# Masking inside the running sum, and VectorE turning the last sixteen keys of each query tile

## The chip, the cores and the metric

The kernel runs on one core of a Trainium2 chip. The metric is the device time of one execution in microseconds. The core's engines have queues of their own: TensorE (PE in the profile; its weight loads are PEld), VectorE (DVE), ScalarE (ACT), GpSimd (POOL) and SyncE (SP, which issues transfers). A profile is one execution recorded instruction by instruction.

## The reference

One layer of a streaming encoder on 512 positions with 16 learned tokens in front (528 keys), width 1024, all in float32. A normalised input is projected to two attention branches of eight heads each; both are merged by gates, projected, added, and followed by a gated feed-forward layer and a last norm. The stick-breaking branch is

```
z = einsum('bhqd,bhkd->bhqk', q, k) * 128 ** -0.5
causal = kpos < qpos
u = where(causal, log_sigmoid(-z), 0)
rest = cumsum(u, axis=3, reverse=True) - u
a = where(causal, exp(log_sigmoid(z) + rest), 0)
o = a @ v
```

So each weight depends on the sum over all later keys that are still before the query, and keys at or behind the query have weight zero. The second branch (differential attention) takes two softmax maps with a bias by distance, subtracts them and weights v in the same way.

## The kernel before

The queries are the 512 real positions, in four tiles of 128; tile t sees the keys 0 to 144 + 128 t. Float32 products are made of three products of split operands (`mm3`, lines 287 to 292: high by high, high by low, low by high).

**The loop over heads.** First eight stick-breaking heads (`sb_head`), then eight differential ones (`df_head`). A head is a generator: it makes its scores, its weights, turns them, and multiplies by v. Each `yield n` lets n units of other work go in between: the projections of the next head's q, k and v, output projections of earlier heads, gates. `weights` prepares the split of projection weights some units ahead (L78 on ScalarE, L79 on VectorE). A planner then fixes each engine's queue: it goes through simulated time and gives a free engine the ready instruction that stands first in the program; instructions inside `tc.high_priority` (evacuations of units) count as 150 places earlier. Only the beginning, up to `order.close()`, is in the order written. On the chip each engine works through its queue in order and waits by semaphores.

**Scores (lines 616 to 626).** Each tile's scores for stick-breaking go to two PSUM tiles of two banks: zA holds tiles 0, 1 (bank 0, columns 0 to 416) and 2 (bank 1), zB tile 3. Each of the four diagonal blocks gets one more product, L620: a bf16 identity times `mask_b`, a constant of 0 and -1e30, which is added to the scores.

**Weights (lines 627 to 641).** s = softplus(z) by three ScalarE activations (L632 to L634) and L635 on VectorE; L639 sums s backwards in place by four scans a head (144, 272, 416 and 528 columns) that add and start from 0; L640 and L641 give exp(z - sum).

**Turning (`attn_out`, lines 545 to 575).** To multiply by v, weights have to lie with keys on the partitions. `turn(j, pt)` transposes key block j of all query tiles that see it on TensorE into one PSUM bank (L556) and splits it into `a_h` (L558, ScalarE) and `a_l` (L559, VectorE). `turn_first` does blocks 0 and 1. One unit later `turn_rest` does block 2 in a third bank, and in a fourth bank `pt` the diagonal block of tile 3 (L568) and the sixteen keys behind each query tile: four small transposes (L571) that place tile t's keys at partitions 32 t. L572 copies the diagonal block to `a_f`; L575 copies the sixteen rows of each tile to `a_s`, two on ScalarE and two on VectorE. Only the last queries of a tile see these keys: 32 in stick-breaking (`lo_rows` 96), 64 in differential heads. `a_s` is zero elsewhere. `weighted` multiplies a_h and a_l with the split v, then a_f (L583) and a_s (L584) with v in plain float32; the matching rows of v come from `v_s` (L537). In a stick-breaking head the four banks are the two halves of two z tiles (from a pool of two), so blocks 0 and 2 share one tile; in a differential head they are four tiles of a pool of four.

**Other parts that matter here.** `bias` (L700, GpSimd) holds a differential head's distance term in the buffer of tag `bias`; L711 on VectorE adds it to the scores. GpSimd's queue also starts many transfers (L145, L690, L801, L803).

Of the kernel before, what the change touches and what calls it, by code (L numbers as in the profile page):

```python
# [9 lines left out]
F32 = mybir.dt.float32  # L10
# [31 lines left out]
def block_kernel(ctx: ExitStack, tc: tile.TileContext, x, meta, norm_mix_g, w_in, w_gate, b_gate,  # L42
# [316 lines left out]
    ident = const.tile([P, P], F32, name="ident")  # L359
    make_identity(nc, ident)  # L360

    mask_b = const.tile([P, 144], BF16, name="mask_b")

    dist = const.tile([P, L], F32, name="dist")
    ident_b = const.tile([P, P], BF16, name="ident_b")
    ones_r = const.tile([P, P], F32R, name="ones_r")
    eps_t = const.tile([P, 1], F32, name="eps_t")
    pcol = const.tile([P, 33], F32, name="pcol")
# [34 lines left out]

    a_s = ap_.tile([P, 256], F32, name="a_s")
    nc.gpsimd.memset(a_s, 0.0)

    def kv_units(key, evac):
        def unit(hf):
# [113 lines left out]
    def v_units(key, d):  # L522
        vT = d["vT"] = ap_.tile([P, L], F32, tag="vT", bufs=1, name="vT")

        def turn():

            vf = ap_.tile([P, 2, P], F32, tag="vf", bufs=2, name="vf")
            vh = ap_.tile([P, 3, P], F32R, tag="vh", bufs=2, name="vh")
            vl = ap_.tile([P, 3, P], F32R, tag="vl", bufs=2, name="vl")
            pt, p5 = tr_tile(), tr_tile()  # L530
            for j in range(4):
                nc.tensor.transpose(pt[:, j * P:(j + 1) * P], vT[:, j * P:(j + 1) * P], ident)  # L532
            pv = pt.rearrange("p (j c) -> p j c", c=P)
            nc.scalar.copy(vh, pv[:, 0:3])
            nc.vector.tensor_tensor(vl, pv[:, 0:3], vh.bitcast(F32), op=ALU.subtract)
            nc.scalar.copy(vf[:, 0], pt[:, 3 * P:4 * P])
            nc.scalar.copy(v_s.rearrange("p (t q) -> p t q", q=32)[:, :, 0:NM],  # L537
                           vT[:, NM:L].rearrange("p (t q) -> p t q", q=P)[:, :, P - NM:P])
            nc.tensor.transpose(p5[:, 0:P], v_s, ident)
            nc.scalar.copy(vf[:, 1], p5[:, 0:P])  # L540
            d["v"] = (vf, vh, vl)

        return kv_units(key, lambda ps, s: nc.scalar.copy(vT[:, s], ps)), turn

    def attn_out(blocks, d, lo_rows, banks):
# [7 lines left out]
        def turn(j, pt):  # L553
            n = 512 - j * P
            for t in range(j, NQ):
                nc.tensor.transpose(pt[:, (t - j) * P:(t - j + 1) * P], blocks(t, j * P, (j + 1) * P), ident)  # L556
            c = slice(off[j], off[j] + n)
            nc.scalar.copy(a_h[:, c], pt[:, 0:n])  # L558
            nc.vector.tensor_tensor(a_l[:, c], pt[:, 0:n], a_h[:, c].bitcast(F32), op=ALU.subtract)  # L559

        def turn_first():
            for j, pt in enumerate(banks()):
                turn(j, pt)

        def turn_rest():
            p2, pt = banks()
            turn(2, p2)
            nc.tensor.transpose(pt[:, 384:512], blocks(3, 3 * P, 4 * P), ident)  # L568
            for t in range(NQ):
                b = blocks(t, (t + 1) * P - 32 * t, (t + 1) * P + NM)  # L570
                nc.tensor.transpose(pt[0:32 * t + NM, t * qn:(t + 1) * qn], b[lo_rows:P], ident[lo_rows:P, lo_rows:P])  # L571
            nc.scalar.copy(a_f, pt[:, 384:512])  # L572
            for t in range(NQ):
                r, c = slice(32 * t, 32 * t + NM), slice(t * qn, (t + 1) * qn)
                (nc.scalar.copy if t < 2 else nc.vector.tensor_copy)(a_s[r, c], pt[r, c])  # L575

        def weighted():
            vf, vh, vl = d["v"]
# [32 lines left out]
    def sb_head(h, d, o_h, o_l):  # L611
# [1 line left out]
        kh, kl = d["k"]  # L613
        zA, zB = z_tile(), z_tile()

        def score(o, t, k0, k1, mo, mn):
            q = slice(t * P, (t + 1) * P)
            mm3(o, [(qh[:, q], ql[:, q], kh[:, k0:k1], kl[:, k0:k1])], stop=(mn == 0))
            if mn:
                nc.tensor.matmul(o[:, mo:mo + mn], lhsT=ident_b, rhs=mask_b[:, 0:mn], start=False, stop=True)  # L620

        score(zA[:, 0, 0:256], 0, 0, 256, NM, P)
        score(zA[:, 0, 144:416], 1, 0, 272, NM + P, P)
        score(zA[:, 1, 0:416], 2, 0, 416, NM + 2 * P, 144)
        score(zB[:, 0, 0:HL], 3, 0, HL, 0, 0)
        score(zB[:, 1, 0:HL], 3, HL, L, 400 - HL, P)
        res = []
        for z, n in ((zA, 416), (zB, HL)):
            zz = z[:, :, 0:n]
# [4 lines left out]
            nc.scalar.activation(e, e, AF.Ln, bias=1.0)  # L634
            nc.vector.scalar_tensor_tensor(s, zz, 0.0, e, op0=ALU.max, op1=ALU.add)  # L635
            sf = s.rearrange("p a b -> p (a b)")
            for a, b in (((0, 144), (144, 416), (416, 832)) if n == 416 else ((0, L),)):
                f = sf[:, a:b][:, ::-1]
                nc.vector.tensor_tensor_scan(f, f, f, 0.0, op0=ALU.add, op1=ALU.bypass)  # L639
            nc.vector.tensor_tensor(s, zz, s, op=ALU.subtract)  # L640
            nc.scalar.activation(s, s, AF.Exp)  # L641
            res.append(sf)
        base = ((0, 0), (0, 144), (0, 416), (1, 0))
        zs = []

        def banks():
            if zs:
                return [z[:, 1] for z in zs]
            zs.extend((z_tile(), z_tile()))
            return [z[:, 0] for z in zs]  # L650

# [45 lines left out]
    def df_head(h, d, o_h, o_l):  # L697
# [53 lines left out]
        yield 1  # L751
        scores3(1)
        maps(3)
        t1, t2, av = attn_out(lambda t, k0, k1: prs[t][:, 0, k0:k1], d, 64, lambda: (tr_tile(), tr_tile()))
        yield 3 if h < NH - 1 else 2
        t1()
        yield 1
# [228 lines left out]
    for k in range(KT):  # L986
# [10 lines left out]
    pm = mm_tile()  # L997
    nc.tensor.transpose(pm[:, 0:33], prow, ident[0:33, 0:33])
    nc.vector.tensor_copy(pcol[:, 8:33], pm[:, 8:33])
    nc.gpsimd.memset(mask_b, 0.0)  # L1000
    nc.gpsimd.affine_select(out=mask_b, in_=mask_b, pattern=[[-1, 144]], compare_op=ALU.is_gt,
                            fill=-BIG, base=0, channel_multiplier=1)
    nc.vector.tensor_copy(ones_r, onesf)
    nc.vector.tensor_copy(ident_b, ident)
    order.close()
    units[5]()
    turn()
# [527 lines left out]
```

## Time and profile before

| | |
|---|---|
| median of 3 runs | 954.66 us (953.51 to 954.71) |
| the profiled execution | 955.27 us |
| its span in the trace | 953.5 us |
| TensorE busy | 940.6 us (99%), granted clock 0.998 |
| VectorE busy | 720.8 us (76%) |
| ScalarE busy | 592.8 us (62%) |
| GpSimd busy | 190.5 us (20%) |
| stick-breaking heads' scans (L639) | from 41.3 us on |
| differential heads, first bias read (L711) | 262.9 us |

A row of a group or of the timeline names the line, the engine, the operation, the tile written and the tiles read, and the shape. Times of products overlap, because they are pipelined; the distance between two starts tells what a product costs when the queue is full. In brackets stands the idle time of the engine ahead of an instruction, and what ended it.

### The profile page before, as it was taken

What the parts mean: (1) busy time and instruction counts of PE and PEld (TensorE: products, weight loads), DVE (VectorE), ACT (ScalarE), POOL (GpSimd) and SP (SyncE); (2) the same over time, 40 slices, a digit from 0 to 9 for tenths busy, and PEclk for the clock granted to TensorE, in tenths of its full rate; (3) what the DMA queues carried; (4) which work ended last, traced back from release to release, by engine and by line L of the source; (5) the groups of instructions that cost most, each with busy time, mean ns of one, the idle gap of its engine ahead of it and who ended that gap; (6) DMA issues with size and microseconds to landing.
All of it is one profiled execution on the core that took longest, in us unless ns stands there. A gap on an engine that the chain in (4) does not pass through costs nothing.

```text
span 953.5 us, 16249 instructions
## 1 busy us (share of the span) xinstructions
PE 940.6 (99%) x6105; PEld 851.1 (89%) x6106; DVE 720.8 (76%) x1336; ACT 592.8 (62%) x1137; POOL 190.5 (20%) x212
## 2 busy tenths in 40 slices
PE   8999999999999999999999999999999999999996
PEld 5988989898999899998987888899999999988886
DVE  7978777765677666876662578899888888989875
ACT  7765676666566666666676356765555555666654
POOL 3200121222133343344513530001000000000013
PEclk9999999999999999999999999999999999999999
DMA  8525678778777879799987865527743343276642
GB/s 246 154 63 149 164 176 204 159 166 228 198 178 174 213 170 185 181 204 180 199 198 168 260 197 170 150 78 171 155 123 111 90 120 103 67 255 203 198 151 89
DMA packets 155824, 158.42 MB, mean 166 GB/s; under 512 B 6465, under 2 KB 117218, under 8 KB 155746
## 3 DMA queue, kind: packets, MB, share of 16 engines
q1 hardware_dynamic: 132690, 101.61, 35.5%
q0 software_dynamic: 22896, 55.72, 28.6%
q8 instruction: 48, 0.79, 0.3%
q14 instruction: 30, 0.25, 0.1%
q10 hardware_dynamic: 160, 0.07, 0.0%
HBM read 133.64 MB, written 50.86 MB: 193 GB/s over the span
## 4 chain that ended last, share of the span: by engine, by line
PE 90%; DVE 6%; ACT 2%; issue 1%; DMA 1%; ACTq 0%; DVEq 0%
PE mm L290 21%; PE mm L291 21%; PE mm L292 21%; PE z L290 6%; PE z L291 6%; PE z L292 6%; PE z L708 1%; PE z L707 1%; DVE wl L79 1%; PE tr L556 1%; PE tr L532 1%; PE z L556 1%; DMA slots<-in_w_ffn_down_dram 1%; PE z L584 1%; DVE hres L1212 1%
## 5 line engine op out<-in xcount | busy, mean ns | idle before, releaser
L290 PE MATMUL mm<-xT_h,wh 128*128 128x264 f32 (+2 forms) x656 | 214.5, 327 | 0.5 <-ACT xT_h L912 0.5
L291 PE MATMUL mm<-xT_l,wh 128*128 128x264 f32 (+2 forms) x656 | 213.4, 325 | 0.5
L292 PE MATMUL mm<-xT_h,wl 128*128 128x264 f32 (+2 forms) x656 | 212.5, 324 | 0.0
L79 DVE TENSOR_TENSOR wl<-wst,wh 128x1024 fp32r<-128x1024 f32 (+1 forms) x147 | 164.2, 1120 | 44.9 <-ACT wh L78 44.7
L78 ACT CAST wh<-wst 128x1024 fp32r<-128x1024 f32 (+1 forms) x147 | 141.6, 965 | 84.7 <-PE mm L291 62.5
L291 PEld LDWEIGHTS mm<-xT_l,wh 128*128 128x128 f32 x656 | 123.5, 188 | 10.1 <-DVE xT_l L913 1.3
L290 PEld LDWEIGHTS mm<-xT_h,wh 128*128 128x128 f32 x656 | 123.5, 188 | 10.0 <-ACT xT_h L912 0.9
L292 PEld LDWEIGHTS mm<-xT_h,wl 128*128 128x128 f32 x656 | 123.4, 188 | 10.0
L290 PE MATMUL mm<-hT_h,wh 128*128 128x256 f32 x304 | 85.7, 284 | 0.4 <-ACT hT_h L1169 0.4
L292 PE MATMUL mm<-hT_h,wl 128*128 128x256 f32 x304 | 86.0, 284 | 0.0
L291 PE MATMUL mm<-hT_l,wh 128*128 128x256 f32 x304 | 86.0, 283 | 0.0
L290 PEld LDWEIGHTS mm<-hT_h,wh 128*128 128x128 f32 x304 | 57.3, 189 | 0.6 <-ACT hT_h L1169 0.6
L291 PEld LDWEIGHTS mm<-hT_l,wh 128*128 128x128 f32 x304 | 57.6, 190 | 0.0
L292 PEld LDWEIGHTS mm<-hT_h,wl 128*128 128x128 f32 x304 | 57.4, 189 | 0.0
L711 DVE CUSTOM_DVE_ANT_0 pr<-z,bias 128x144 f32<-128x144 f32 (+3 forms) x64 | 30.9, 501 | 35.0 <-PE z L708 34.9
L290 PE MATMUL mm<-o_h,wh 128*128 128x512 f32 x128 | 53.2, 416 | 0.0
L1437 POOL TENSOR_TENSOR outs<-hres,gF 128x512 f32<-128x512 f32 x4 | 6.2, 1554 | 226.0 <-DVE hres L1423 217.8
L291 PE MATMUL z<-wl,da 128*128 128x512 f32 (+1 forms) x132 | 50.4, 381 | 0.3 <-DVE wl L79 0.3
L145 POOL DMA_DIRECT2D ds<-in_w_ffn_down_dram x36 | 30.1, 840 | 102.3 <-ACT wh L78 68.6
L291 PE MATMUL mm<-o_l,wh 128*128 128x512 f32 x128 | 50.1, 392 | 0.3 <-DVE o_l L779 0.3
L290 PE MATMUL z<-wh,da 128*128 128x512 f32 (+1 forms) x132 | 50.2, 381 | 0.0
L292 PE MATMUL z<-wh,da 128*128 128x512 f32 (+1 forms) x132 | 50.2, 380 | 0.0
(375 smaller groups left out, 2554.4 us busy)
## 6 DMA issues: line engine op xcount, KB each, us to landing
wst<-in_w_in_dram SPq DMA_DIRECT2D x40, 512.0 KB, 5.7
ds<-in_w_ffn_down_dram POOLq DMA_DIRECT2D x30, 512.0 KB, 6.2
wst<-in_w_ffn_gate_dram SPq DMA_DIRECT2D x22, 512.0 KB, 4.0
wsu<-in_w_ffn_up_dram SPq DMA_DIRECT2D x20, 512.0 KB, 3.8
wst<-in_w_gate_dram SPq DMA_DIRECT2D x16, 512.0 KB, 6.8
y_df<-y_out POOLq DMA_DIRECT2D x32, 256.0 KB, 7.4
slots<-ds SPq DMA_DIRECT2D x13, 512.0 KB, 3.4
os<-in_w_out_dram POOLq DMA_DIRECT2D x12, 512.0 KB, 5.4
```

Source lines behind the costliest of these rows:

```text
L78: cast["last"] = (hi_copy or nc.scalar.copy)(hi, src)
L79: (lo_eng or nc.vector).tensor_tensor(lo, src, hi.bitcast(F32), op=ALU.subtract)
L145: tc.add_manual_dep(nc.gpsimd.dma_start(dst, src, **kw).ins, cast["last"].ins.name, paced)
L290: nc.tensor.matmul(ps, lhsT=ah, rhs=bh, start=(start and i == 0), stop=False, skip_group_check=skip)
L291: nc.tensor.matmul(ps, lhsT=ah, rhs=bl, start=False, stop=False, skip_group_check=skip)
L292: nc.tensor.matmul(ps, lhsT=al, rhs=bh, start=False, stop=(stop and i == n - 1), skip_group_check=skip)
L532: nc.tensor.transpose(pt[:, j * P:(j + 1) * P], vT[:, j * P:(j + 1) * P], ident)
L556: nc.tensor.transpose(pt[:, (t - j) * P:(t - j + 1) * P], blocks(t, j * P, (j + 1) * P), ident)
L584: nc.tensor.matmul(ps.rearrange("p (t q) -> p t q", q=P)[:, :, lo_rows:P], lhsT=vf[:, 1], rhs=a_s[:, 0:4 * qn], start=False, stop=True)
L707: nc.tensor.matmul(o, lhsT=q[c][:, qs], rhs=k[c][:, 0, k0:k1], start=True, stop=False)
L708: nc.tensor.matmul(o, lhsT=q[c][:, qs], rhs=k[c][:, 1, k0:k1], start=False, stop=True)
L711: nc.vector.tensor_tensor_reduce(po, zz, bb, scale=1.0, scalar=-3.0e38, op0=ALU.add, op1=ALU.max, accum_out=mx[:, t, c:c + 1])
```

## The change

**The mask.** L620, `mask_b` and `ident_b` go. A new constant `resets` (128 by 528, float32) is 1 everywhere but for a 0 in column 399 + p of row p. The scan now forms state = resets * state + s, from the last key to the first, and starts from 1e30: keys behind the diagonal keep a sum of about 1e30, so that exp gives zero, and at the 0 the sum starts afresh. The scan of tile 2 covers 400 columns instead of 416. `resets` is filled on GpSimd and VectorE at the beginning, and takes the one buffer of tag `bias`, so that the first differential head's bias can be written only when the last scan has read it.

**The sixteen keys.** The four small transposes on TensorE (L571) and the four copies (L575) go. At the end of `turn_first` VectorE turns blocks of 32 by 32 from the weights in SBUF straight into `a_s`: one for each tile in a stick-breaking head, two in a differential head. Each block takes the 32 keys that end with the sixteen; the sixteen in front of these meet zeros, because `v_s` now has its rows in the second half of each 32. The diagonal block's transpose (L568) moves into the bank of block 2, ahead of the split; `turn_rest` needs one bank instead of two.

```diff
-        def score(o, t, k0, k1, mo, mn):
+        def score(o, t, k0, k1):
             q = slice(t * P, (t + 1) * P)
-            mm3(o, [(qh[:, q], ql[:, q], kh[:, k0:k1], kl[:, k0:k1])], stop=(mn == 0))
-            if mn:
-                nc.tensor.matmul(o[:, mo:mo + mn], lhsT=ident_b, rhs=mask_b[:, 0:mn], start=False, stop=True)
+            mm3(o, [(qh[:, q], ql[:, q], kh[:, k0:k1], kl[:, k0:k1])])
...
-            for a, b in (((0, 144), (144, 416), (416, 832)) if n == 416 else ((0, L),)):
+            for a, b in (((0, 144), (144, 416), (416, 816)) if n == 416 else ((0, L),)):
                 f = sf[:, a:b][:, ::-1]
-                nc.vector.tensor_tensor_scan(f, f, f, 0.0, op0=ALU.add, op1=ALU.bypass)
+                nc.vector.tensor_tensor_scan(f, resets[:, L - (b - a):][:, ::-1], f, BIG, op0=ALU.mult, op1=ALU.add)
...
-            nc.scalar.copy(v_s.rearrange("p (t q) -> p t q", q=32)[:, :, 0:NM],
+            nc.scalar.copy(v_s.rearrange("p (t q) -> p t q", q=32)[:, :, 32 - NM:32],
...
             for t in range(j, NQ):
                 nc.tensor.transpose(pt[:, (t - j) * P:(t - j + 1) * P], blocks(t, j * P, (j + 1) * P), ident)
+            if j == 2:
+                nc.tensor.transpose(pt[:, 384:512], blocks(3, 3 * P, 4 * P), ident)
...
         def turn_first():
-            for j, pt in enumerate(banks()):
+            for j, pt in enumerate(banks(2)):
                 turn(j, pt)
+            for t in range(NQ):
+                b = blocks(t, (t + 1) * P - 32 + NM, (t + 1) * P + NM)
+                for i in range(qn // 32):
+                    nc.vector.transpose(a_s[32 * t:32 * t + 32, t * qn + 32 * i:t * qn + 32 * i + 32],
+                                        b[lo_rows + 32 * i:lo_rows + 32 * i + 32])
 
         def turn_rest():
-            p2, pt = banks()
+            p2 = banks(1)[0]
             turn(2, p2)
-            nc.tensor.transpose(pt[:, 384:512], blocks(3, 3 * P, 4 * P), ident)
-            for t in range(NQ):
-                b = blocks(t, (t + 1) * P - 32 * t, (t + 1) * P + NM)
-                nc.tensor.transpose(pt[0:32 * t + NM, t * qn:(t + 1) * qn], b[lo_rows:P], ident[lo_rows:P, lo_rows:P])
-            nc.scalar.copy(a_f, pt[:, 384:512])
-            for t in range(NQ):
-                r, c = slice(32 * t, 32 * t + NM), slice(t * qn, (t + 1) * qn)
-                (nc.scalar.copy if t < 2 else nc.vector.tensor_copy)(a_s[r, c], pt[r, c])
+            nc.scalar.copy(a_f, p2[:, 384:512])
...
-    nc.gpsimd.memset(mask_b, 0.0)
-    nc.gpsimd.affine_select(out=mask_b, in_=mask_b, pattern=[[-1, 144]], compare_op=ALU.is_gt,
-                            fill=-BIG, base=0, channel_multiplier=1)
+    nc.gpsimd.memset(resets, 1.0)
+    nc.vector.tensor_scalar(resets[:, 399:399 + P], ident, -1.0, 1.0, op0=ALU.mult, op1=ALU.add)
     nc.vector.tensor_copy(ones_r, onesf)
-    nc.vector.tensor_copy(ident_b, ident)
```

More of the change, by code (lines that the diff above doesn't have):

```diff
@@ L360, in block_kernel @@
     make_identity(nc, ident)
-    mask_b = const.tile([P, 144], BF16, name="mask_b")
     dist = const.tile([P, L], F32, name="dist")
-    ident_b = const.tile([P, P], BF16, name="ident_b")
     ones_r = const.tile([P, P], F32R, name="ones_r")
@@ L405, in block_kernel @@
     nc.gpsimd.memset(a_s, 0.0)
+    resets = ap_.tile([P, L], F32, tag="bias", name="resets")
     def kv_units(key, evac):
@@ L614, in sb_head @@
         zA, zB = z_tile(), z_tile()
-        def score(o, t, k0, k1, mo, mn):
+        def score(o, t, k0, k1):
             q = slice(t * P, (t + 1) * P)
-            mm3(o, [(qh[:, q], ql[:, q], kh[:, k0:k1], kl[:, k0:k1])], stop=(mn == 0))
-            if mn:
[L620 to L626, printed above, removed]
+            mm3(o, [(qh[:, q], ql[:, q], kh[:, k0:k1], kl[:, k0:k1])])
+        score(zA[:, 0, 0:256], 0, 0, 256)
+        score(zA[:, 0, 144:416], 1, 0, 272)
+        score(zA[:, 1, 0:416], 2, 0, 416)
+        score(zB[:, 0, 0:HL], 3, 0, HL)
+        score(zB[:, 1, 0:HL], 3, HL, L)
         res = []
@@ L644, in sb_head, with banks @@
         zs = []
-        def banks():
-            if zs:
-                return [z[:, 1] for z in zs]
+        def banks(n):
+            if n == 1:
+                return [zs[0][:, 1]]
             zs.extend((z_tile(), z_tile()))
@@ L753, in df_head @@
         maps(3)
-        t1, t2, av = attn_out(lambda t, k0, k1: prs[t][:, 0, k0:k1], d, 64, lambda: (tr_tile(), tr_tile()))
+        t1, t2, av = attn_out(lambda t, k0, k1: prs[t][:, 0, k0:k1], d, 64, lambda n: [tr_tile() for _ in range(n)])
         yield 3 if h < NH - 1 else 2
```

## The prediction

> **What bounds the kernel now.** I read the page first: the engines' shares and the chain of work that ended last.
>
> ```profile
> span 953.5 us, 16249 instructions
> ...
> PE 940.6 (99%) x6105; PEld 851.1 (89%) x6106; DVE 720.8 (76%) x1336; ACT 592.8 (62%) x1137; POOL 190.5 (20%) x212
> ...
> PE 90%; DVE 6%; ACT 2%; issue 1%; DMA 1%; ACTq 0%; DVEq 0%
> ```
>
> TensorE (PE) is busy for 99% of the span and holds 90% of the chain. Shares are averages over stages, so the next view is the busy time by stretch. The two stretches below hold the stick-breaking heads from the middle of head 0 on, and the differential heads; after the stretch come its length and then the busy time of PE, weight load, VectorE (DVE), ScalarE (ACT) and GpSimd (POOL).
>
> ```profile
> 54.00:259.00 205.00, 204.96 (x1346) 184.44 (x1347) 146.50 (x229) 132.41 (x251) 39.14 (x52) 1.00 0.69 172
> 259.00:496.00 237.00, 237.00 (x1527) 215.16 (x1525) 164.10 (x432) 157.34 (x370) 89.74 (x99) 1.00 0.86 190
> ```
>
> From 54 to 496 us PE has no idle time, at a granted clock of 1.00, while VectorE has 58 and 73 us to spare. The view of the waits, limited to PE, has one entry in the attention heads, once, in head 0:
>
> ```profile
> PE z L556 <- DVE a_l L559: 0.7, 1, 0.7
> ```
>
> So what leaves PE's queue behind 54 us should leave the time. What leaves it before (the four masks of head 0, from 35 us on) only lengthens that wait; I count it as nothing, although it would be worth half a microsecond if VectorE weren't late there.
>
> **The masks on PE (L620).** How often the mask product runs, and the timeline of PE around one of them (start, duration, line):
>
> ```profile
> L620 PE MATMUL z<-mask_b,ident_b x32: 229/230/237, 35.1 to 235.4; 128*128 128x128 bf16 x24, 128*128 128x144 bf16 x8
> ```
>
> ```profile
> 93.46 0.28 PE L292 MATMUL z<-kh,ql 128*128 128x256 f32 x1
> 93.58 0.23 PE L620 MATMUL z<-mask_b,ident_b 128*128 128x128 bf16 x1
> 93.61 0.37 PE L290 MATMUL z<-kh,qh 128*128 128x272 f32 x1
> 93.82 0.29 PE L291 MATMUL z<-kl,qh 128*128 128x272 f32 x1
> 93.95 0.28 PE L292 MATMUL z<-kh,ql 128*128 128x272 f32 x1
> ```
>
> Durations overlap here, since products are pipelined, so I take starts. From the start of the mask to the second product behind it 0.24 us pass; one product of this size alone takes 0.12 to 0.13 (93.82 to 93.95). The mask costs 0.12 us, although the step to its follower is only 0.03: the rest falls on that follower, which starts and then runs 0.37 instead of 0.29. Seven heads with four masks: 28 x 0.12 = 3.4 us.
>
> The Trainium skill, "TensorE: Matmul & The Clock Gate", section "Back-to-back issue gap", gives 134 cycles of 2.4 GHz (56 ns) for 128 columns, and about 60 cycles (25 ns) up to 64. By it the masks would be worth 1.6 us, the 64 small transposes 1.6, and the time after would be about 951.5. The row disagrees with it in this place (0.12), and the row goes into my sum.
>
> **The small transposes on PE (L571), and the diagonal block (L568).** First the end of the second turning in a stick-breaking head, with a place where ordinary transposes pass into products of 512 columns:
>
> ```profile
> 112.20 0.38 PE L556 MATMUL z<-ident,s 128*128 128x128 f32 x2
> 112.51 0.33 PE L568 MATMUL z<-ident,s 128*128 128x128 f32 x1
> 112.77 0.32 PE L571 MATMUL z<-ident,s 32*16 32x32 f32 x4
> 113.02 0.50 PE L290 MATMUL mm<-o_h,wh 128*128 128x512 f32 x1
> 113.35 0.39 PE L291 MATMUL mm<-o_l,wh 128*128 128x512 f32 x1
> ...
> 117.88 0.60 PE L532 MATMUL tr<-ident,vT 128*128 128x128 f32 x4
> 118.31 0.27 PE L539 MATMUL tr<-ident,v_s 128*128 128x128 f32 x1
> 118.34 0.48 PE L290 MATMUL mm<-o_h,wh 128*128 128x512 f32 x1
> 118.66 0.40 PE L291 MATMUL mm<-o_l,wh 128*128 128x512 f32 x1
> ```
>
> Before: 112.20 to 113.35, 1.15 us. After, the diagonal block is the third of three equal transposes at 0.11 each (117.88 to 118.31 for four), and the last passes into the products as at 118.31: 2 x 0.11 + 0.35 = 0.57. Saved: 0.58 us. Heads 1 to 6 look like this; in heads 0 and 7 the order is a little different (in head 0 the small ones stand between unit products, in head 7 the diagonal block follows directly), and I estimate 0.1 less each (0.48), for the step of 0.31 ahead of L568 above, 0.09 more than two transposes take: 6 x 0.58 + 0.96 = 4.4 us.
>
> In a differential head, where the four small ones are 64 wide:
>
> ```profile
> 315.46 0.38 PE L556 MATMUL tr<-ident,pr 128*128 128x128 f32 x2
> 315.68 0.27 PE L568 MATMUL tr<-ident,pr 128*128 128x128 f32 x1
> 315.88 0.39 PE L571 MATMUL tr<-ident,pr 64*16 64x64 f32 x4
> 316.20 0.66 PE L532 MATMUL tr<-ident,vT 128*128 128x128 f32 x4
> 316.70 0.27 PE L539 MATMUL tr<-ident,v_s 128*128 128x128 f32 x1
> ```
>
> Before: 315.46 to 316.70, 1.24 us for eleven instructions. After: seven full transposes at 0.11, 0.77. Saved 0.47; eight heads, 3.8 us.
>
> **VectorE: the scan and the new transposes.** Groups of VectorE by line; the last numbers are count, total and mean ns of one:
>
> ```profile
> L639 DVE TENSOR_TENSOR_SCAN s<-s 128x528 f32<-128x528 f32 x8 | 9.9, 1233 | 0.0
> ...
> L640 DVE TENSOR_TENSOR s<-z,s 128x528 f32<-128x528 f32 x8 | 5.6, 697 | 0.0
> L635 DVE SCALAR_TENSOR_TENSOR s<-z,e 128x528 f32<-128x528 f32 x8 | 5.6, 695 | 0.0
> ...
> L711 DVE DVE_READ_ACCUMULATOR2_ANT mx<- 128x1 f32 x64 | 5.2, 82 | 0.0
> ...
> L575 DVE COPY a_s<-tr 16x64 f32<-16x64 f32 x16 | 3.6, 226 | 0.4
> ...
> L559 DVE TENSOR_TENSOR a_l<-z,a_h 128x256 fp32r<-128x256 f32 x8 | 3.3, 413 | 0.0
> ...
> L575 DVE COPY a_s<-z 16x32 f32<-16x32 f32 x16 | 3.1, 193 | 0.4
> ```
>
> The scan already reads two operands; now the first is another tile and both operations work. No row shows that form. A second operation is free elsewhere (695 against 697), so one end is no change (the third stretch loses 16 of 416 columns, nothing to speak of); the other is half as much again, 0.6 us for 528 columns and 1.6 for a head's 1344. I take no change.
>
> No row shows a VectorE transpose. The nearest small instructions are the copies it replaces (0.19 and 0.23); the bounds are 0.08 (a read of the accumulator) and 0.41 (256 columns). I take 0.2. That adds 4 x 0.2 and takes 2 x 0.19 in a stick-breaking head, adds 8 x 0.2 and takes 2 x 0.23 in a differential one: 0.4 and 1.1 us, 12 us in all, against 131 us idle. ScalarE loses two copies a head. Where the transposes stand in VectorE's queue matters more:
>
> ```profile
> 109.57 1.23 DVE L79 TENSOR_TENSOR wl<-wst,wh 128x1024 fp32r<-128x1024 f32 x1 [0.48 <-ACT wh L78]
> ...
> 111.31 1.14 DVE L559 TENSOR_TENSOR a_l<-z,a_h 128x512 fp32r<-128x512 f32 x2
> ```
>
> ```profile
> 313.09 1.22 DVE L79 TENSOR_TENSOR wl<-wst,wh 128x1024 fp32r<-128x1024 f32 x1 [1.76 <-ACT wh L78]
> 314.35 1.16 DVE L559 TENSOR_TENSOR a_l<-tr,a_h 128x512 fp32r<-128x512 f32 x2
> ```
>
> They need only the finished weights, as the first turning on PE does, so they add no new wait. In the program they stand behind both a_l, where an L79 and the third a_l would go back by 0.4 to 1.1 us with nobody waiting; or the planner puts them into holes like the 0.48 and 1.76 in brackets. Both cost PE nothing. If that cover is gone (ahead of the first a_l, behind the hole), the second turning is late: its bank shares a tile with the one that this a_l reads, and it starts 0.2 us after that a_l ends (111.31 + about 0.68, against 112.20).
>
> **Setup and GpSimd.** The new constant takes one fill and one VectorE instruction, like the old ones. But it lives in the buffer of the differential heads' bias, whose first filling now runs early:
>
> ```profile
> 32.67 5.26 POOL L700 TENSOR_SCALAR bias<-dist 128x528 f32<-128x528 f32 x1
> ```
>
> ```profile
> 242.97 1.00 DVE L640 TENSOR_TENSOR s<-z,s 128x832 f32<-128x832 f32 x1
> ```
>
> ```profile
> 262.95 0.31 DVE L711 CUSTOM_DVE_ANT_0 pr<-z,bias 128x144 f32<-128x144 f32 x1 [2.09 <-PE z L708]
> ```
>
> It has to move behind the last scan, which ends at about 243, and is first read at 263: 20 us for an instruction of at most 5.3, with GpSimd's transfers queued behind it. I count nothing.
>
> **Sum**, against this execution's 955.27 us (span 953.5 and 1.8 around it): 955.3 - 3.4 - 4.4 - 3.8 = 943.7. The median of the runs, 954.66, is 0.6 lower: 943.1.
>
> **Rivals.**
> (1) Only the removed products' own steps go, and their neighbours keep the gaps. Own steps: 0.03 a mask (93.58 to 93.61), 0.25 for the four small ones (112.77 to 113.02), 0.32 in the differential heads (315.88 to 316.20): 0.8 + 2.0 + 2.6 = 5.4 us, 949.3. Against it: the follower of a mask runs longer than its sisters, which it should not do without the mask.
> (2) Slower: VectorE turns the blocks ahead of the first a_l. With a price x each, PE is late by 4x - 0.2 in a stick-breaking head. In a differential head 8x meets the 0.4 us to 315.46 (314.35 + 0.69, against 315.46) and, since the second turning there has a bank of its own, about 1 us more before its products read a_l: 8x - 1.5. Over eight heads each, 96x - 13.6: 5.6 us at 0.2, and the whole gain of 11.6 from x = 0.26. At 0.3 it is 15.2, and the time 958.3. For it: no row excludes 0.3. Against it: program order, and the holes. The Trainium skill, "VectorE: DVE Perf Modes", section "Two Vector instructions with no wait between them", speaks for a high price: an instruction that starts in another group of 32 partitions than the last is held until all earlier ones have finished, and each new transpose reads or writes another group than its neighbours; no row here shows it for a transpose.
> (3) Another wait takes the gain: weights or transfers arrive late once PE is faster by 2.6%. Then the time stays within 1.5 us of 954.66, say 953.9. Against it: the brackets show VectorE waiting for ScalarE's L78, not PE for either.
> (4) The scan grows by half: 1.6 us more before the weights are ready, so the first turning may stall by up to 1 us in eight heads: 951.
>
> **Chances.** Forecast 0.66, with its own range 941.5 to 946; (1) 0.12; (2) 0.09; (3) 0.08; (4) 0.05. The range is 941 to 951: it leaves out (2), (3) and a little on both sides. This kernel's measurement tells about 0.2% (1.9 us) from no change. Faster: forecast, (1) and (4), 0.83; same: (3), 0.08; slower: (2), 0.09.
>
> **What would show it.** Right: no L620; four products in a row of 0.12 across the old mask's place; 0.57 from the first of three transposes to the second product; PE still without idle time from 55 us to the end of the heads; VectorE's transposes near 0.2; the scan of 528 columns near 1.23. Wrong: idle time of PE ahead of L556 or L290 with a_l or the transposes as releaser (2), a follower that keeps 0.37 (1), a longer scan (4).

## The result and the profile after

The changed kernel takes 949.08 us (median of six runs, 945.69 to 950.57) against 954.57 for the kernel before on the same chip (953.51 to 954.71): a ratio of 0.9938, with a 95% interval of 0.9926 to 0.9949. That is 5.5 us less. The forecast was 943.1, which would have been 11.5 less: the direction was right, and half of the gain is missing. The profiled execution took 949.31 us, with a span of 947.5.

The page of the changed kernel, the rows that answer to those of before:

```profile
span 947.5 us, 16049 instructions
...
PE 929.5 (98%) x6009; PEld 843.6 (89%) x6010; DVE 733.9 (77%) x1400; ACT 586.3 (62%) x1105; POOL 186.8 (20%) x211
...
PE 76%; DVE 12%; issue 4%; ACT 3%; DMA 3%; POOL 1%; SPq 0%; POOLq 0%; ACTq 0%; DVEq 0%
```

PE's own busy time fell by 11.1 us (940.6 to 929.5). That this is close to the forecast is luck: a faster feed-forward stage and a stretch at half clock, both below, enter it, and nobody had forecast either. The span fell by 6.0 only, and the chain shows where to look: PE fell from 90% to 76%, VectorE doubled from 6% to 12%. PE now waits. The view of the waits, limited to PE:

```profile
PE mm L292 <- DVE wl L79: 3.3, 1, 3.3
PE z L555 <- DVE a_l L560: 1.5, 2, 1.0
PE mm L290 <- ACT qx L1317: 0.8, 1, 0.8
```

The first and the third were not there before; the second was there once, with 0.7 us. To see what each stage gave or took, I paired the products of PE in both traces and followed by how much the later one is ahead. The lead is taken from the two profiled executions:

| stretch (us of before) | lead gained | what happens there |
|---|---|---|
| to 54 | -0.95 | 0.4 at the start; 0.5 at head 0's second turning, where PE waits 1.03 instead of 0.74 |
| 54 to 493 | +9.9 | the heads: masks and turnings; the lead is now 8.98 |
| 493 to 531 | -0.5 | end of the heads |
| 531 to 546 | -5.3 | merge of the branches: the wait on wl, and a slow PE behind it |
| 546 to 640 | +0.4 | output product and second normalisation |
| 640 to 828 | +3.1 | feed-forward stage, where the diff touches nothing |
| 828 to 850 | -1.2 | the wait on qx (L1317) and a small one behind it |
| the rest | +0.5 | the last stores |
| all | +6.0 | |

So from 54 us on the heads gave 9.9 of the 11.6 that were forecast, the merge took 5.3 back, and the feed-forward stage gave 3.1 that nobody had looked for.

**The heads, as forecast.** The timeline of PE across the place of the old mask, then the second turning of a stick-breaking head (behind the last product of its neighbour), then that of a differential head:

```profile
92.85 0.28 PE L292 MATMUL z<-kh,ql 128*128 128x256 f32 x1
92.97 0.29 PE L290 MATMUL z<-kh,qh 128*128 128x272 f32 x1
93.09 0.29 PE L291 MATMUL z<-kl,qh 128*128 128x272 f32 x1
...
110.96 0.28 PE L292 MATMUL mm<-xT_h,wl 128*128 128x264 f32 x1
111.34 0.44 PE L555 MATMUL z<-ident,s 128*128 128x128 f32 x2
111.62 0.27 PE L557 MATMUL z<-ident,s 128*128 128x128 f32 x1
111.64 0.47 PE L290 MATMUL mm<-o_h,wh 128*128 128x512 f32 x1
111.96 0.39 PE L291 MATMUL mm<-o_l,wh 128*128 128x512 f32 x1
...
309.69 0.38 PE L555 MATMUL tr<-ident,pr 128*128 128x128 f32 x2
...
310.45 0.27 PE L538 MATMUL tr<-ident,v_s 128*128 128x128 f32 x1
```

The steps of 0.12 are there, and the follower lasts 0.29 instead of 0.37. The differential head needs 0.76 for its seven transposes (0.77 forecast). In the stick-breaking head the step from 110.96 to 111.34 is 0.38 where 0.12 would do: PE stands there for 0.26.

VectorE's groups of the scan and of the new transposes (count, total and mean ns):

```profile
L568 DVE STREAM_TRANSPOSE a_s<-pr 32x32 f32<-32x32 f32 x64 | 13.0, 204 | 1.6
L636 DVE TENSOR_TENSOR_SCAN s<-resets,s 128x528 f32<-128x528 f32 x8 | 9.9, 1234 | 0.0
...
L568 DVE STREAM_TRANSPOSE a_s<-s 32x32 f32<-32x32 f32 x32 | 6.6, 205 | 0.5
```

Both prices were right: 0.204 us for a transpose (0.2), 1234 ns for the scan of 528 columns (1233 before).

**The heads, what was missed.** VectorE's queue ahead of that late turning:

```profile
106.77 0.86 DVE L568 STREAM_TRANSPOSE a_s<-s 32x32 f32<-32x32 f32 x4
...
108.87 1.22 DVE L79 TENSOR_TENSOR wl<-wst,wh 128x1024 fp32r<-128x1024 f32 x1
110.01 0.68 DVE L600 SCALAR_TENSOR_TENSOR ql<-mm,qh 128x512 fp32r<-128x512 f32 x1
110.61 1.15 DVE L560 TENSOR_TENSOR a_l<-z,a_h 128x512 fp32r<-128x512 f32 x2
```

The four transposes stand ahead of everything up to a_l. They fill the hole of 0.48 ahead of L79 and push the rest back by what exceeds it. Heads 1 to 5 lose 0.26, 0.27, 0.29, 0.62 and 0.27 us in this way, 1.7 together, which is what the 9.9 lack of 11.6.

**The merge.** First the order of the two VectorE instructions that matter in the kernel before, then VectorE, GpSimd and PE in the changed kernel:

```profile
536.10 1.23 DVE L79 TENSOR_TENSOR wl<-wst,wh 128x1024 fp32r<-128x1024 f32 x1
538.51 0.69 DVE L1131 TENSOR_TENSOR mf<-sg 128x512 f32<-128x512 f32 x1 [1.18 <-POOL sg L1127]
```

```profile
532.68 2.32 DVE L1126 TENSOR_TENSOR mf<-sg 128x512 f32<-128x512 f32 x1 [1.62 <-POOL sg L1122]
534.92 1.21 DVE L79 TENSOR_TENSOR wl<-wst,wh 128x1024 fp32r<-128x1024 f32 x1
```

```profile
531.34 1.31 POOL L1122 TENSOR_TENSOR sg<-sg,y_df 128x512 f32<-128x512 f32 x1
...
533.17 1.27 POOL L1122 TENSOR_TENSOR sg<-sg,y_sb 128x512 f32<-128x512 f32 x1
```

```profile
532.54 0.40 PE L291 MATMUL mm<-xT_l,wh 128*128 128x512 f32 x1
536.19 0.80 PE L292 MATMUL mm<-xT_h,wl 128*128 128x512 f32 x1 [3.25 <-DVE wl L79]
536.78 0.63 PE L290 MATMUL mm<-xT_h,wh 128*128 128x512 f32 x1
537.21 0.63 PE L291 MATMUL mm<-xT_l,wh 128*128 128x512 f32 x1
```

The planner has turned the order round. The sum of the block f = 0 (L1126) now stands ahead of the split of the next gate weights (L79); it has to wait for GpSimd's product of that block, and PE waits for the split behind it. Behind the wait, products of 512 columns come every 0.43 us instead of 0.23 until 539: the granted clock is 0.5 there.

### The profile page after: what moved, and what is told of

Read it like the earlier page. It is cut to its first block, busy times and chain, and to the rows that moved or that the text cites. A ratio compares the mean times of both kernels' runs of the same rounds, so it can differ in the third digit from the quotient of the medians.

```text
span 947.5 us, 16049 instructions
## 1 busy us (share of the span) xinstructions
PE 929.5 (98%) x6009; PEld 843.6 (89%) x6010; DVE 733.9 (77%) x1400; ACT 586.3 (62%) x1105; POOL 186.8 (20%) x211
## 4 chain that ended last, share of the span: by engine, by line
PE 76%; DVE 12%; issue 4%; ACT 3%; DMA 3%; POOL 1%; SPq 0%; POOLq 0%; ACTq 0%; DVEq 0%
PE mm L292 17%; PE mm L291 17%; PE mm L290 17%; PE z L290 6%; PE z L291 6%; PE z L292 6%; DVE wl L79 3%; DVE s L636 2%; PE z L705 1%; PE z L704 1%; ACT wh L78 1%; PE tr L555 1%; DMA wsu<-in_w_in_dram 1%; DVE s L637 1%; DVE s L632 1%
## 5 line engine op out<-in xcount | busy, mean ns | idle before, releaser
L79 DVE TENSOR_TENSOR wl<-wst,wh 128x1024 fp32r<-128x1024 f32 (+1 forms) x147 | 166.4, 1136 | 31.1 <-ACT wh L78 30.7
L290 PEld LDWEIGHTS mm<-xT_h,wh 128*128 128x128 f32 x656 | 124.0, 189 | 10.4 <-ACT xT_h L909 0.9
L291 PEld LDWEIGHTS mm<-xT_l,wh 128*128 128x128 f32 x656 | 123.8, 189 | 10.4 <-DVE xT_l L910 1.3
L292 PE MATMUL mm<-o_h,wl 128*128 128x512 f32 x128 | 50.2, 392 | 0.0
```

What stands on the lines that cost most here:

```text
L79: (lo_eng or nc.vector).tensor_tensor(lo, src, hi.bitcast(F32), op=ALU.subtract)
L290: nc.tensor.matmul(ps, lhsT=ah, rhs=bh, start=(start and i == 0), stop=False, skip_group_check=skip)
L291: nc.tensor.matmul(ps, lhsT=ah, rhs=bl, start=False, stop=False, skip_group_check=skip)
L292: nc.tensor.matmul(ps, lhsT=al, rhs=bh, start=False, stop=(stop and i == n - 1), skip_group_check=skip)
```

## The experiments

**The two halves alone.** Each half of the diff was put into the kernel before. The two old bf16 constants stay allocated in both, so that all tiles keep their addresses.

The core of the mask alone:

```diff
-        score(zA[:, 0, 0:256], 0, 0, 256, NM, P)
+        score(zA[:, 0, 0:256], 0, 0, 256)
...
+                nc.vector.tensor_tensor_scan(f, resets[:, L - (b - a):][:, ::-1], f, BIG, op0=ALU.mult, op1=ALU.add)
```

The core of the turning alone:

```diff
-                nc.tensor.transpose(pt[0:32 * t + NM, t * qn:(t + 1) * qn], b[lo_rows:P], ident[lo_rows:P, lo_rows:P])
+                    nc.vector.transpose(a_s[32 * t:32 * t + 32, t * qn + 32 * i:t * qn + 32 * i + 32],
+                                        b[lo_rows + 32 * i:lo_rows + 32 * i + 32])
...
```

> The kernel before with the first half of the change alone: the mask in the scan, the turning left to PE. The two bf16 constants stay allocated, unused, so that all addresses are those of the kernel before. Theory A (each removed mask product gives back the step it took, and the planner's order in the merge of the branches stays as before): a lead of PE over the kernel before that grows by 0.55 us in each of the heads 1 to 7, 3.9 us at 490 us, no wait on wl at 530 to 545 us, median 954.6 - 3.9 = 950.7 us. Rival B (this half already brings the bad order in the merge): the same lead at 490 us, and a wait of about 3 us with the half clock behind it that takes 3 to 5 us of it: 954 to 956.

> The kernel before with the second half of the change alone: VectorE turns the sixteen keys behind each query tile, the masks stay with PE. Addresses are those of the kernel before. Theory A (the second turning gives back 0.52 us in a stick-breaking head and 0.45 in a differential one, and VectorE's transposes ahead of the first a_l take some 1.7 us of it in heads 1 to 5): a lead of 6 x 0.52 + 0.9 + 8 x 0.45 - 1.7 - 0.9 (the beginning) = 5.0 us at 490 us; with the order of before in the merge the median is 949.6, with the bad order 953 to 955. Rival B (the transposes make PE late only together with the mask's half, whose scan has a second operand): no gaps of 0.38 us ahead of the second turning, a lead of 6.7 at 490 us.

The mask alone: 951.18 us against 954.49, a ratio of 0.9965 (0.9955 to 0.9976). The lead of PE grows by 0.10 to 0.13 at each mask, some 0.48 in each of heads 1 to 7, from 0.24 at 57 us to 3.57 at 493, and there is no wait in the merge. Theory A, but 3.3 us where it had 3.9; the prediction's 3.4 was nearer.

The turning alone: 955.19 us, a ratio of 1.0005 (0.9996 to 1.0014), no gain at all, though PE is ahead by 6.99 us at 493 us. Its differential heads give 3.8 (lead 3.16 to 6.99), just the forecast; its stick-breaking heads, where the second turning comes 0.23 to 0.29 late in five of them, give 2.9 (lead 0.30 to 3.16) instead of 4.4. So the late turnings come without the mask's half too (theory A, not rival B); that the lead is 6.99 where A had 5.0 is mostly the start, which gave 0.3 where A had put a loss of 0.9. Then the merge takes it all:

```profile
PE mm L292 <- DVE wl L79: 3.8, 1, 3.8
```

Busy times in the merge (stretch, length, PE, PEld, DVE, ACT, POOL, granted clock, DMA share, GB/s), the mask alone and then the turning alone:

```profile
530.00:545.00 15.00, 15.00 (x68) 12.43 (x67) 7.93 (x11) 6.29 (x12) 8.17 (x8) 1.00 0.89 271
```

```profile
530.00:545.00 15.00, 11.05 (x38) 8.31 (x37) 8.35 (x10) 5.83 (x10) 7.74 (x8) 0.77 0.88 258
```

So the bad order in the merge comes with the half that concerns the turning, some 40 us behind the last head in which it changes an instruction (493 to 532 us).

**The order in the merge.** The sum of block f = 0 is tied behind the split of the gate's block 5, which is the order of before.

```diff
+        if f == 0:
+            prepare(prep_at["gate", 0, 5] + 1)
...
-        nc.vector.tensor_tensor(m, sg[0], sg[1], op=ALU.add)
+        total = nc.vector.tensor_tensor(m, sg[0], sg[1], op=ALU.add)
+        if f == 0:
...
+            tc.add_manual_dep(total.ins, cast["wl", at_of["gate", 0, 5]].ins.name, behind)
```

> The changed kernel with one instruction of VectorE held back: in the merge of the branches, the sum of the third block (f = 0) waits until the low half of the weights of the gate's block 5 is split, which is the order of the kernel before. Everything else stands as in the changed kernel. Theory A (the order of these two instructions costs the lost time of this stage: PE stands 3.3 us on wl, and the 3.4 us after that run at a granted clock of 0.5, which costs some 1.9 more): no wait of PE above 0.5 us on wl between 525 and 545 us, granted clock 1.00 there, median 949.1 - 5.2 = 943.9 us. Rival B (PE is fed too slowly in this stage whatever the order: VectorE is the bound there and the wait only moves to the next weights): a wait of about 3 us within the next 20 us, median 948.5 to 949.5. Rival C (the half clock does not come of the wait): the wait is gone, the half clock stays at about 536 us, median 949.1 - 3.3 = 945.8.

947.69 us (945.02 to 949.98), a ratio of 0.9926 (0.9911 to 0.9941): 3.8 above A's 943.9. In the profiled execution the wait is gone and the clock is 1.00, as A has it; PE is ahead of the changed kernel by 4.5 us at 540 us, of which 2.5 are lost again by 603, in the later sums of the merge and the output's first products (two waits of 0.46 and 0.40, the rest in smaller steps). The executions spread over 5 us, and their interval overlaps that of the changed kernel (0.9926 to 0.9949). So the trace shows the mechanism, and the time doesn't prove it.

**The transposes behind a_l.** In the stick-breaking heads VectorE's transposes wait for the last a_l of the first two turnings.

```diff
-            nc.vector.tensor_tensor(a_l[:, c], pt[:, 0:n], a_h[:, c].bitcast(F32), op=ALU.subtract)
+            d["a_l"] = nc.vector.tensor_tensor(a_l[:, c], pt[:, 0:n], a_h[:, c].bitcast(F32), op=ALU.subtract)
...
+                    tr = nc.vector.transpose(a_s[32 * t:32 * t + 32, t * qn + 32 * i:t * qn + 32 * i + 32],
...
+                    if lo_rows == 96:
...
+                        tc.add_manual_dep(tr.ins, d["a_l"].ins.name, behind)
```

> The changed kernel, with VectorE's transposes of the stick-breaking heads tied behind the last a_l of the first two turnings, so that they no longer stand ahead of the first a_l in VectorE's queue. Theory A (the four transposes of 0.205 us ahead of a_l make PE late at the second turning, by 0.26 to 0.62 us in each of heads 1 to 5): the gap ahead of that turning's products is 0.12 us in all heads, PE is earlier by about 1.7 us at the end of the heads, median 947.4 us. Rival B (the transposes then stand in front of what the weighting needs, or of the next head's splits, and the wait moves there): PE no earlier at 493 us, median 949 or more.

945.98 us, a ratio of 0.9908 (0.9896 to 0.9921). The same place in PE's timeline:

```profile
110.71 0.28 PE L292 MATMUL mm<-xT_h,wl 128*128 128x264 f32 x1
110.83 0.38 PE L555 MATMUL z<-ident,s 128*128 128x128 f32 x2
...
111.39 0.40 PE L291 MATMUL mm<-o_l,wh 128*128 128x512 f32 x1
```

The step ahead of the turning is 0.12, and from there to the second product pass 0.56 (0.57 forecast). PE is ahead of the changed kernel by 1.9 us at 193 us. Theory A. The medians are 3.1 apart; the merge may have given the rest, for in this execution the wait on wl is there (3.52 us) but the granted clock behind it stays at 1.00.

**Both edits.** The two diffs above together.

> The changed kernel with both of the earlier edits: the sum of block f = 0 behind the low half of the weights of the gate's block 5, and the transposes of the stick-breaking heads behind the last a_l. Theory A (the two losses are apart from each other and add): the lead of the one edit at 493 us (1.9 us over the changed kernel) and that of the other at 540 to 845 us (2.7) are both there, median between 949.1 - 1.9 - 2.7 = 944.5 and, if the half clock stays away in most executions, 942.5 us. Rival B (an earlier PE only waits longer in the merge, where DMA and ScalarE bring the gates' first parts): median 946 as with the transposes' edit alone.

946.17 us, a ratio of 0.9908 (0.9893 to 0.9923), no better than with the transposes' edit alone: rival B's time, but not for rival B's reason. VectorE, GpSimd and PE in the merge:

```profile
528.73 3.85 DVE L79 TENSOR_TENSOR wl<-wst,wh 128x1024 fp32r<-128x1024 f32 x1 [0.62 <-ACT wh L78]
```

```profile
528.40 1.31 POOL L1126 TENSOR_TENSOR sg<-sg,y_df 128x512 f32<-128x512 f32 x1
529.63 0.58 POOL L1142 DMA_DIRECT2D hres<-in_x_dram  x1
530.22 1.27 POOL L1126 TENSOR_TENSOR sg<-sg,y_sb 128x512 f32<-128x512 f32 x1
```

```profile
532.64 0.50 PE L293 MATMUL mm<-xT_h,wl 128*128 128x512 f32 x1 [2.57 <-DVE wl L79]
```

The split now stands in front of the sum and starts in time, but it lasts 3.85 us instead of 1.23: it ends 1.1 us after GpSimd's second product. GpSimd works without a break from 528.40 to 531.49 (two products and the start of a transfer between them), and the split, which began at 528.73, needs about its usual 1.23 us after that: next to nothing of it was done before. In the run with the order's edit alone, the split began first:

```profile
531.86 1.23 DVE L79 TENSOR_TENSOR wl<-wst,wh 128x1024 fp32r<-128x1024 f32 x1 [0.78 <-ACT wh L78]
```

```profile
532.37 1.85 POOL L1123 TENSOR_TENSOR sg<-sg,y_df 128x512 f32<-128x512 f32 x1
```

There it took its 1.23 us, and GpSimd's product took 1.85 instead of 1.3. The Trainium skill, "SBUF — State Buffer", section "Who interferes with whom", states that a VectorE instruction with two inputs in SBUF contends with a GpSimd instruction that reads SBUF, and that the order of issue decides which of the two is blocked. These rows agree, and so does the sum of 2.32 us (0.69 elsewhere) in the changed kernel, which began at 532.68 while GpSimd was at work from 531.34 to 534.44.

**GpSimd out of the way.** The transposes' edit stays; in the merge it is now GpSimd's second product for f = 0 that waits for the split, and the sum with it.

```diff
-            (nc.gpsimd if f < 6 else nc.vector).tensor_tensor(sg[br], sg[br], y, op=ALU.mult)
+            gated = (nc.gpsimd if f < 6 else nc.vector).tensor_tensor(sg[br], sg[br], y, op=ALU.mult)
+            if f == 0 and br == 1:
+                prepare(prep_at["gate", 0, 5] + 1)
...
+                tc.add_manual_dep(gated.ins, cast["wl", at_of["gate", 0, 5]].ins.name, behind)
```

> The changed kernel with the transposes of the stick-breaking heads behind the last a_l, as before, and in the merge GpSimd's second product for the block f = 0 (its differential branch) tied behind the low half of the weights of the gate's block 5 on VectorE; so the sum of that block stands behind these weights too, and GpSimd does not work while VectorE splits them. Theory A (what PE waits for in the merge is this one split, made late once by the sum in front of it and once, with the sum out of the way, by GpSimd's products beside it, which stretched it from 1.23 to 3.85 us): the split takes 1.2 to 1.3 us, no wait of PE above 0.5 us on wl between 520 and 545 us, granted clock 1.00 there, median 943 to 944 us (946.0 to 946.2 with the transposes' edit and the wait still there, less a wait of 2.6 to 3.5, plus up to 1 us that comes back in the merge's later sums). Rival B (the merge gives the time back at its later blocks): no gain over 946.

943.73 us (942.4 to 946.58), a ratio of 0.9894 (0.988 to 0.9908): 11.1 us less than the kernel before, the lowest median of all versions. Its interval overlaps that of the transposes' edit alone (0.9896 to 0.9921), so here too the trace shows the mechanism, and the time alone doesn't prove the further gain. The split and the merge:

```profile
527.06 1.23 DVE L79 TENSOR_TENSOR wl<-wst,wh 128x1024 fp32r<-128x1024 f32 x1 [0.82 <-ACT wh L78]
```

```profile
530.00:545.00 15.00, 15.00 (x64) 11.45 (x63) 8.62 (x12) 6.22 (x10) 7.45 (x6) 1.00 0.80 261
```

The split takes 1.23, PE has no idle time, the clock is 1.00. Theory A. In all five executions the granted clock is 0.997 to 0.999 over the whole span, as in the kernel before; in the six of the changed kernel it is 0.994 to 0.998.

**The feed-forward stage: addresses.** The change takes out 544 bytes of constants, so the tiles behind them move down by 544. Four kernels move tiles and nothing else: the changed kernel with 544, 32 or 512 unused bytes, and the kernel before with its constants moved away (all other tiles as in the changed kernel). A fifth puts 32 bytes in front of the kernel before. The unused tile has 136, 8 or 128 columns of 4 bytes.

```diff
+    const.tile([P, 136], F32, name="pad_c")
...
-    mask_b = const.tile([P, 144], BF16, name="mask_b")
...
-    ident_b = const.tile([P, P], BF16, name="ident_b")
...
+    both_b = ap_.tile([P, 2 * L], BF16, tag="bias", name="both_b")
+    mask_b, ident_b = both_b[:, 0:144], both_b[:, 144:272]
```

> The changed kernel with an unused tile of 544 bytes a partition, the size of the two constants that the change took out, so that every tile behind it has its old address again (0 instead of 32 modulo 64 bytes). The order of the instructions is that of the changed kernel. Theory A (the faster products of the feed-forward stage come of the tiles' addresses): its 256-column products on t_h and t_l follow each other at 118 to 119 ns again instead of 113 to 115, and the median is 949.1 + 3.3 = 952.4 us. Rival B (they come of something else that the change did, the work beside them or the order): products at 113 to 115 ns, median 949.1.

> The kernel before with an unused tile of 32 bytes a partition in front, so that its tiles lie at 32 modulo 64 bytes as in the changed kernel; the order of the instructions is that of the kernel before. Theory A (addresses): the feed-forward products on t_h and t_l at 113 to 115 ns instead of 118 to 119, median 954.6 - 3.3 = 951.3 us. Rival B: nothing moves, 954.6.

> The kernel before with its two bf16 constants moved into the buffer of the heads' bias, where the change keeps its own constant; all other tiles then have the addresses of the changed kernel (544 bytes lower), and the computation and the order of its products are those of before. Theory A (the addresses alone make the feed-forward stage faster): products on t_h and t_l at 113 to 116 ns instead of 118 to 119, median 954.6 - 3.5 = 951.1 us. Rival B (the addresses act only together with what the change did): nothing moves, 954.6.

> The changed kernel with an unused tile of 32 bytes: the tiles on the left stand 512 bytes lower than in the kernel before and at 0 modulo 64. Theory A (the place within 64 bytes decides the speed of the feed-forward products): the products on t_h and t_l at 118 to 119 ns, 952 to 953 us. Theory B (the greater part of the shift, 512 bytes, decides, with a boundary that the tiles crossed or left): 113 to 116 ns, about 949.

> The changed kernel with an unused tile of 512 bytes: the tiles on the left stand 32 bytes lower than in the kernel before and at 32 modulo 64. Theory A (the place within 64 bytes): products on t_h and t_l at 113 to 116 ns, about 949 us. Theory B (the 512 bytes): 118 to 119 ns, 952 to 953.

How many products PE runs from 650 to 800 us tells the kernels apart in one number. The kernel before, the changed kernel, and the kernel before with its constants moved:

```profile
650.00:800.00 150.00, 150.00 (x1259) 150.00 (x1259) 127.33 (x198) 82.42 (x136) 4.31 (x5) 1.00 0.48 125
```

```profile
650.00:800.00 150.00, 150.00 (x1283) 150.00 (x1282) 129.09 (x201) 83.92 (x137) 4.33 (x5) 1.00 0.48 126
```

```profile
650.00:800.00 150.00, 150.00 (x1283) 150.00 (x1282) 129.66 (x201) 83.84 (x137) 4.31 (x5) 1.00 0.47 125
```

| kernel | tiles moved by | products, 650 to 800 us | us (ratio to before) |
|---|---|---|---|
| before | 0 | 1259 | 954.57 (1) |
| before, 32 in front | +32 | 1260 | 954.59 (1.0, 0.9991 to 1.0009) |
| changed, 544 in front | 0 | 1259 | 952.96 (0.9982, 0.9973 to 0.9991) |
| changed, 32 in front | -512 | 1259 | 953.33 (0.9977, 0.9961 to 0.9992) |
| changed, 512 in front (two executions) | -32 | 1283 | 949.4 (0.9946, 0.9928 to 0.9964) |
| changed | -544 | 1283 | 949.08 (0.9938, 0.9926 to 0.9949) |
| before, constants moved | -544 | 1283 | 950.58 (0.9964, 0.9951 to 0.9976) |

The addresses alone make the kernel before faster by 3.9 us, and without them the changed kernel is only 1.7 faster. In both, theory A holds (952.96 and 950.58, where it had 952.4 and 951.1). The slow and the fast pace, twelve products on t_h and t_l in the kernel before (703.65 to 705.07, 118 ns each) and with its constants moved (701.54 to 702.90, 113 ns):

```profile
703.65 0.28 PE L290 MATMUL z<-t_h,wh 128*128 128x256 f32 x1
...
705.07 0.28 PE L290 MATMUL mm<-hT_h,wh 128*128 128x256 f32 x1
```

```profile
701.54 0.28 PE L290 MATMUL z<-t_h,wh 128*128 128x256 f32 x1
...
702.90 0.28 PE L290 MATMUL mm<-hT_h,wh 128*128 128x256 f32 x1
```

The runs with 32 and 512 bytes in front of the changed kernel agree with the place within 64 bytes (their theory A). But 32 bytes up in the kernel before (954.59, where theory A had 951.3) does not do what 32 bytes down does in the changed one, so the place within 64 bytes is not the rule. Modulo 128 bytes the fast kernels had the moving tile t at 96 and the weights at 32; the last run tried the rule that 64 bytes between the two operands make a product fast, with the tiles of hT, on top of the best version.

```diff
-    hT_h, hT_l = (xtp.tile([P, NM + KT * SEQ], F32R, tag=t, name=n)[:, NM:]...
+    hT_h, hT_l = (xtp.tile([P, 2 * NM + KT * SEQ], F32R, tag=t, name=n)[:, 2 * NM:]...
```

> The kernel with the transposes of the stick-breaking heads behind the last a_l and GpSimd's product behind the split (GpSimd's edit), with hT_h and hT_l 64 bytes further within their tiles; nothing else moves and the order is the same. Worked out from the earlier runs: modulo 128 bytes the moving operand t and the weights w stood at (96, 64) in the kernel before, (96, 96) with 32 bytes in front, (96, 32) in the changed kernel, the one with 512 bytes and the one before with its constants moved; only at (96, 32), 64 bytes apart, the products on t came at 113 to 116 ns, else at 118 to 119. hT and w stood at equal remainders in all of them (64 and 64, 96 and 96, 32 and 32), and the products on hT came at 117 to 120 everywhere. Theory A (what counts is that the moving operand and the weights lie 64 bytes apart modulo 128): with hT at 96 and the weights at 32 its some 880 products in the feed-forward stage come at 113 to 116 ns instead of 117 to 120, 880 x 4.5 ns = 4 us, median 943.7 - 4 = 939.7 us. Rival B (it is something else about t or the weights, or hT is slow for another reason): products on hT at 117 to 120 ns, median 943.7.

945.44 us, a ratio of 0.9896 (0.9878 to 0.9914), where theory A had 939.7, and 1276 products from 650 to 800 us. Worked out from the starts of consecutive products, those on hT came every 118 ns instead of 119 to 120, and those on t, whose addresses had not moved, slowed down from 113 to 115 to 117 or 118. The rule falls: how fast the products on t are depends on where hT lies too. Which relation decides stays open. The time tells no more, because the merge lost 1.7 us in this execution (a transfer of y_df that GpSimd waited for came 1.9 us later).

## Why the prediction was right, and where it was wrong

The direction was right, and so were the prices in the heads, but for the late turnings. That the time lies within 941 to 951 is luck: two things that the prediction did not have, the merge (5.3 us lost) and the tiles' places (3.9 us gained), partly cancel. With the tiles at their old places the same change takes 952.96 us, above the range.

- **The masks, 3.4 us.** Right: 3.3, in the medians and in the lead.
- **The differential turnings, 3.8.** Right: 3.8.
- **The stick-breaking turnings, 4.4.** The products did what was forecast (0.56 to the second product where PE isn't late). The step that failed is "Both cost PE nothing". Holes and program order were named as the cover, and the planner put the transposes ahead of a hole that is smaller than they are (0.48 against 0.86). That is the place of rival (2), with its x at 0.2: it counted 0.6 a head, and 0.26 to 0.62 were lost, 1.7 in all. In the differential heads, where the holes are larger, nothing was lost. With the transposes behind a_l the loss is gone.
- **The scan and the price of a transpose.** Right: 1234 ns and 0.204 us. The rule of the Trainium skill ("VectorE: DVE Perf Modes", section "Two Vector instructions with no wait between them") did not make the price high: four transposes in a row take 0.86 us, 0.215 each. By that rule each of them is held, so no row shows what one costs without it.
- **The first 54 us, counted as nothing.** 0.95 lost in the profiled execution. 0.5 goes at head 0's second turning, which waits for a_l longer than it did; the mask alone loses the same 0.5 there (the lead falls from 0.48 to -0.01) and the turning alone nothing, so it comes with the mask's half. The rest is the start, which differs by up to 1.0 between profiled executions of versions that do the same there (a lead of -0.60 at 35 us in the changed kernel, 0.45 in the best version).
- **"So what leaves PE's queue behind 54 us should leave the time."** This step cost most. It was read off the heads, where PE had no idle time, and carried to the end of the kernel without a look at the stages behind them. In the merge VectorE, GpSimd and PE meet within a few us, in an order that the planner makes. Rival (3), weights that arrive late once PE is faster, comes nearest, but its price was a guess for the whole gain and not worked out at this place: 3.3 us of wait, and some 1.9 of half clock behind it. Its reason isn't what the runs show: in the best version PE is 11 us ahead in the merge and doesn't wait for these weights at all. What makes the wait is the order on VectorE, and GpSimd's products beside the split, not PE's speed alone.
- **Not on the list at all:** the 3.9 us from the addresses. They make the best version's 943.73 look more like the forecast 943.1 than it is. In its profiled execution (942.4 us) PE is ahead of the kernel before by 0.1 us at 54 us, 11.65 at 493, 10.4 at 640, 13.2 at 828 and 12.4 at the end. So the heads, with the late turnings mended, give 11.55 of the 11.6. Then 1.3 go between 493 and 640 (0.5 at the end of the heads, as in the changed kernel, the rest in steps of 0.1 to 0.3 whose cause stays open) and 0.8 behind the feed-forward stage, where PE waits for qx of ScalarE (1.1 us in two waits). 2.9 come in the feed-forward stage, where the kernel before gained 3.5 by its moved constants alone. The best version at the old places was not run.

## What to carry to other kernels

A gain read off one stage is kept only if no later stage makes PE wait: follow the instructions behind the changed stage to the end, above all where three engines meet. When a planner sets the order, a few instructions more or fewer can turn round two others far away; compare the orders, and tie the pair that counts. And hold the addresses when a constant is taken out, or the measurement mixes two changes: here the tiles' places were worth 3.9 us, more than either half of the diff was in the time.

## What the runs showed of the hardware that was not expected

- **Addresses.** The place of unchanged tiles sets the pace of 256-column products: 113 ns or 118 for the same product, 1283 or 1259 of them in 150 us. Which relation between the operands decides wasn't found; two rules were tried and fell.
- **VectorE beside GpSimd.** A VectorE subtraction of two SBUF tiles took 3.85 us instead of 1.23 beside two GpSimd products.
- **The clock.** Waits of PE of 1.96, 2.57, 2.88, 3.25 and 3.80 us in the merge were followed by a granted clock of 0.5 for 3.41 or 6.83 us (512 bytes in front, both edits, 544 bytes in front, the changed kernel, the turning alone), and waits of 3.52 and 3.57 us by none (the transposes' edit, 32 bytes in front of the changed kernel). The traces' clock records show what decides. In them the granted clock changes only at whole steps of 3.41 us: in the changed kernel 529.07 us at 1.00 (155 steps), then 3.41 at 0.5, then 406.19 at 1.00 (119 steps). Where at least 1.96 us of PE's idle time fell into one such step (1.96, 2.57, 2.16, 2.97 and 2.05 in the five runs), the next step ran at 0.5. Where the wait was parted between two steps (1.67 and 1.85; 1.91 and 1.66), the clock stayed. So in these runs the limit lies near 1.9 us of idle time in one step, and it counts where in the steps a wait falls. The Trainium skill, "TensorE: Matmul & The Clock Gate", section "What's actually happening", has the clock halved after an idle window of about 3.4 us that runs freely. The length of the steps agrees; that a step has to be idle as a whole does not.
- **The spread.** The executions of kernels with this wait spread by 2.6 to 5.5 us, those of the kernel before and of the mask alone by 1.0 to 2.4; with the wait mended it is still 4.2 (GpSimd out of the way) to 5.0 (the order's edit), so the wait is not all of it.
